# The experts' gate, x times sigmoid of 1.702 x, as one activation in place of a sigmoid and a product

## The chip, the cores and the metric

The kernel runs on one core of a Trainium2 chip. A core has a matrix engine (TensorE, PE in the profile; its weight loads are PEld) and three engines for the rest: VectorE (DVE), ScalarE (ACT) and GpSimd (POOL). SyncE (SP) issues most of the transfers (DMA). Each engine works through its own list of instructions in order and waits on semaphores for the others. The metric is the device time of one execution in microseconds (us), the median of several runs.

## The reference, cut to what matters

One encoder layer: attention, then a mixture of experts. 1024 tokens of width 1024 go to 4 of 32 experts each; every expert has a gate half and an up half of 1024 columns and a product back down. The part that the change touches is one line:

```python
def expert_block(args):
    xb, e = args
    gu = xb @ w_gate_up[e] + b_gate_up[e]
    gate = jnp.minimum(gu[:, :D_FF], SWIGLU_LIMIT)
    up = jnp.clip(gu[:, D_FF:], -SWIGLU_LIMIT, SWIGLU_LIMIT)
    glu = gate * jax.nn.sigmoid(SWIGLU_ALPHA * gate)      # SWIGLU_ALPHA = 1.702
    return ((up + 1.0) * glu) @ w_down[e] + b_down[e]
```

## The kernel before

The program runs in stages: projections and attention (to about 500 us), output projection and routing (to about 700), the experts (about 620 to 2240), and a final normalisation. The experts' first visit begins while the last tiles are still routed.

**Visits.** The experts are ranked by how many tokens they got, and a plan (PLAN) holds a capacity for each rank. Each expert is visited once or more. A visit of several blocks of 128 tokens is of kind H (`accH`, `xH`, `hH`), one of a single block of kind L (`accL`, `xL`, `hL`). The two streams are merged beforehand into one sequence of steps (`merged`), by estimated costs of TensorE and bytes moved. A step is a quarter of a 512-column piece of an expert's weights: kind "g" for gate and up columns, "d" for the product down.

**Weights.** SyncE loads two steps' weights at a time (L1181 for gate and up, L1184 for down). Most visits compute in a split form: a weight is "cooked" (`cook`) into a high part by ScalarE (L1305) and a low part, weight minus high part, which VectorE (736 of 1024 elements per partition, 368 of 512 columns twice) and GpSimd (the other 288) compute together (L1307). TensorE then does three products: high by high, high by low, low by high (L1532 to L1534 for wide visits, L236 to L238 for blocks over 64 tokens). So L238 and L1534 are the ones that need L1307. Blocks of up to 64 tokens alone take the weights as they are (L1557). Ten buffers hold raw and cooked weights; a load waits until L1307 has read the buffer before it.

**Gates.** In wide visits `glu_w` works on one quarter (j) of the columns with tokens along the row: VectorE adds the bias and clips (L1425, or L1422 and L1423 where high and low product lie side by side), ScalarE takes the sigmoid (L1428), VectorE multiplies it by the clipped gate (L1429). For the up half VectorE clips and multiplies (L1434) and the result is split again for the product down. In other visits `glu` does the same by blocks of 512 columns: L1449 and L1451 add, L1456 clips, L1457 is the sigmoid, L1458 the product, L1461 and L1462 the up half. `leave` scales a block's output (L1484, L1486 to L1489) and GpSimd adds it to the tokens' rows in memory (L1490).

**Order.** The source order is the input of a scheduler which simulates the program and sets each engine's list by that; the changed kernel is scheduled anew. SyncE's order is fixed by hand.

**Ranking.** `rank` (L1188 on) counts, sorts and writes the experts' order to `ord_i` (L1210); SyncE reads it before it can load the next experts' lists and weights. It runs on VectorE between the first visit's gates.

**The end.** A loop over leftover blocks (L1640), whose count is computed on the chip, is empty in this execution. `finish` loads tile i (L1709), squares it and takes a root on ScalarE (L1712, L1713), scales on VectorE (L1714, L1715) and stores (L1716). ScalarE's functions come in tables; a table load stands in its list where the function of the next instruction is in another one.

Of the kernel before, what the change touches and what calls it, by code (L numbers as in the profile page):

```python
# [9 lines left out]
AF = mybir.ActivationFunctionType  # L10
ALU = mybir.AluOpType
# [13 lines left out]
ALPHA = 1.702  # L25
# [48 lines left out]
def span(v):  # L74

    return sum(b[1] for b in v[2]) if len(v[2]) > 1 else 0


def joined(v):

    return 0 < span(v) <= 208


def groups(v, nt):

    return (0,) if nt > 64 else (0, 64) if nt > 32 else (0, 32, 64, 96) if plain(v) else (0, 32)
# [140 lines left out]
class Kernel:  # L227
# [1019 lines left out]
    def experts(self):  # L1247
# [3 lines left out]
        V, A, P, T = nc.vector, nc.scalar, nc.gpsimd, nc.tensor  # L1251
# [122 lines left out]
        def parts(name, n):  # L1374

            st, r, blocks = vis[n]
            if st == "H":
                t = wp.tile([128, 2 * KD * WIDE], F32R, name=name + st)  # L1380
            else:
                t = lp.tile([128, 2048], F32R, name=name + st)
            sp = span(vis[n])
            out, at = [], 0
            if plain(vis[n]):
                nt = blocks[0][1]
                w = t.bitcast(F32)[:, 0:KD * nt].rearrange("p (k t) -> p k t", k=KD)
                return w, [(w, w, None)]
            if sp and name == "x":
                w = t[:, 0:2 * KD * sp].rearrange("p (u k t) -> p u k t", u=2, k=KD)  # L1390
                return w, [(None, w[:, 0, :, o - blocks[0][0]:o - blocks[0][0] + nt],
                            w[:, 1, :, o - blocks[0][0]:o - blocks[0][0] + nt]) for o, nt in blocks]
            full = sum(b[1] for b in blocks if b[1] > 64)
            w = t[:, 0:2 * KD * full].rearrange("p (u k t) -> p u k t", u=2, k=KD) if full else None
            for o, nt in blocks:
                if nt > 64:
                    out.append((None, w[:, 0, :, at:at + nt], w[:, 1, :, at:at + nt]))
                    at += nt
                else:
                    lo = groups(vis[n], nt)[1]  # L1400
                    q = t[:, 2 * KD * full:2 * KD * full + KD * (lo + nt)].rearrange("p (k t) -> p k t", k=KD)
                    if nt < lo:
                        P.memset(q[:, :, nt:lo].bitcast(F32), 0.0)
                    out.append((q, q[:, :, 0:nt], q[:, :, lo:lo + nt]))
            return w, out
# [7 lines left out]
        def glu_w(n, c, j, p):  # L1413

            sp = span(vis[n])
            kk = 4 * (c // 2) + j
            bc = biases[n][:, 8 * (c % 2) + kk:8 * (c % 2) + kk + 1]
            top = LIM + c % 2
            t = wp.tile([128, 512], F32, name="t", bufs=3)[:, :sp]
            if joined(vis[n]):  # L1420
                A.activation(t, p[:, sp:2 * sp], AF.Copy)
                V.scalar_tensor_tensor(t, p[:, :sp], bc, t, op0=ALU.add, op1=ALU.add)  # L1422
                V.tensor_scalar(t, t, top, None, op0=ALU.min)  # L1423
            else:
                V.tensor_scalar(t, p[:, :sp], bc, top, op0=ALU.add, op1=ALU.min)  # L1425
            if c % 2 == 0:
                a = gates[n, j] = wp.tile([128, WIDE], F32, name="ga", bufs=5)[:, :sp]
                A.activation(a, t, AF.Sigmoid, scale=ALPHA)  # L1428
                V.tensor_tensor(a, a, t, op=ALU.mult)  # L1429
                return  # L1430
            if kk == 0:
                hs[n] = parts("h", n)
            a = gates.pop((n, j))
            V.scalar_tensor_tensor(a, t, 1.0 - LIM, a, op0=ALU.max, op1=ALU.mult)  # L1434
            w, blocks = hs[n]
            full = w.shape[3]
            self.split(w[:, 0, kk, :full], w[:, 1, kk, :full], a[:, :full])
            if full < sp:
                _, hi, lo = blocks[-1]
                self.split(hi[:, kk, :], lo[:, kk, :], a[:, full:])  # L1440

        def glu(b, p, c):

            nt = b["nt"]
            t = wp.tile([128, 512], F32, name="t", bufs=3)[:nt]
            c0 = 1024 * (c % 2) + 512 * (c // 2)
            bv = biases[b["n"]][:, c0:c0 + 512]
            *more, o = groups(vis[b["n"]], nt)
            V.tensor_tensor(t, p[o:o + nt], bv[o:o + nt], op=ALU.add)  # L1449
            for o in more:  # L1450
                V.tensor_tensor(t, p[o:o + nt], t, op=ALU.add)  # L1451
            if c % 2 == 0:
                if len(late) == 2:
                    settle(*late[0][1:3])
                a = b["a"] = lp.tile([128, 512], F32, name="a", bufs=3)[:nt]
                V.tensor_scalar(t, t, LIM, None, op0=ALU.min)  # L1456
                A.activation(a, t, AF.Sigmoid, scale=ALPHA)  # L1457
                V.tensor_tensor(a, a, t, op=ALU.mult)  # L1458
                return
            a = b.pop("a")  # L1460
            V.tensor_scalar(t, t, LIM, -LIM, op0=ALU.min, op1=ALU.max)  # L1461
            V.scalar_tensor_tensor(a, t, 1.0, a, op0=ALU.add, op1=ALU.mult)  # L1462
            if c == 1:
                hs[b["n"]] = parts("h", b["n"])

            late.append((self.pe_time + 5.0, b, c // 2, a))

        def settle(b=None, f=-1):

            for x in list(late):  # L1470
                if x[0] <= self.pe_time or (x[1] is b and x[2] <= f):
                    late.remove(x)
                    turn(x[3], hs[x[1]["n"]][1][x[1]["j"]][1:], x[1]["nt"], 4 * x[2])
# [32 lines left out]
        def mm(m):  # L1506
# [12 lines left out]
            if kind == "g" and span(vis[n]):  # L1519
                sp = span(vis[n])  # L1520
                x = xs[n][0]
                if kh == 0:
                    accs[n] = [bank() for _ in range(4)]
                for j in range(4):
                    ws = slice(128 * j, 128 * j + 128)
                    p = accs[n][j]
                    for k in range(KP):
                        kk = KP * kh + k
                        if joined(vis[n]):
                            mm(p[:, :2 * sp], hi[:, k, ws], x[:, :, kk, :], start=kk == 0, stop=False)  # L1530
                        else:
                            mm(p[:, :sp], hi[:, k, ws], x[:, 0, kk, :], start=kk == 0, stop=False)  # L1532
                            mm(p[:, :sp], hi[:, k, ws], x[:, 1, kk, :], start=False, stop=False)  # L1533
                        mm(p[:, :sp], lo[:, k, ws], x[:, 0, kk, :], start=False, stop=kk == 7)  # L1534
                    if kh == NP - 1:
                        glu_w(n, c, j, p)
                self.pe_time += pe_cost(vis[n], "g")
                settle()
                return
# [202 lines left out]
```

## Time and profile before

| | |
|---|---|
| time, median of 3 runs | 2270.0 us (2266.41 to 2276.21) |
| the profiled execution's own time | 2269.73 us |
| its span, first to last instruction | 2268.0 us |
| TensorE busy | 2084.2 us, 92% of the span |
| VectorE busy | 1568.2 us, 69% |
| ScalarE busy | 949.6 us, 42% |
| GpSimd busy | 1111.3 us, 49% |
| DMA | 579.17 MB, mean 255 GB/s |

The 1.7 us between span and time lie around the program. Busy shares are means over stages with different limits, and TensorE's busy time includes some of the time in which its pipeline waits; so what a part of a stage is worth is read in that stage. A line of idle time names who ended it. All rows are of one execution.

### The profile page before, as it was taken

To read this page: it belongs to the slowest core of one execution; us is meant where nothing else is said; L and a number is where in the kernel's file an instruction comes from. 1 tells how busy PE (TensorE), PEld (TensorE's weight loads), DVE (VectorE), ACT (ScalarE), POOL (GpSimd) and SP (SyncE) were. 2 spreads that over 40 slices of the span, in tenths; PEclk is the share of its full clock that TensorE was granted. 3 is DMA by queue.
4 is the path that set the end of the run, shared out by engine and by line. 5 is a ranking of instruction groups with operands and counts; after the bars stand their busy time and mean duration, and the time that the engine had idled before them with its cause. 6 is when DMAs were issued, how large, how long until landed. Compare 5 with 4: busy or idle time off the path is not lost. (4 is left out here: it accounts for less than half of the span.)

```text
span 2268.0 us, 34804 instructions
## 1 busy us (share of the span) xinstructions
PE 2084.2 (92%) x12090; PEld 1533.8 (68%) x12090; DVE 1568.2 (69%) x2790; ACT 949.6 (42%) x1612; POOL 1111.3 (49%) x959
## 2 busy tenths in 40 slices
PE   6999999999787998888879999999999999999973
PEld 3987777777576876665546555566686777877772
DVE  3777646876585699787866454455686868878975
ACT  3543436764353456554643121222233434345543
POOL 2522123543555567778874334333536455555453
PEclk8999999999899999999989999999999999999987
DMA  9555577823556699898879998999898898898775
GB/s 320 157 166 149 163 217 198 159 78 124 152 164 191 233 298 307 278 293 256 299 225 368 371 320 292 344 347 329 263 347 265 309 315 307 304 313 298 257 251 188
DMA packets 325114, 579.17 MB, mean 255 GB/s; under 512 B 40009, under 2 KB 78089, under 8 KB 322577
## 3 DMA queue, kind: packets, MB, share of 16 engines
q1 hardware_dynamic: 301529, 524.22, 67.7%
q0 software_dynamic: 23408, 52.71, 11.2%
q8 instruction: 97, 1.59, 0.3%
q14 instruction: 80, 0.66, 0.1%
HBM read 518.23 MB, written 58.92 MB: 254 GB/s over the span
## 5 line engine op out<-in xcount | busy, mean ns | idle before, releaser
L1307 POOL TENSOR_TENSOR w<-w,w 128x288 fp32r<-128x288 f32 x456 | 599.9, 1366 | 547.7 <-ACT w L1305 523.6
L1305 ACT ACTIVATE w<-w 128x1024 fp32r<-128x1024 f32 x456 | 469.1, 1054 | 525.3 <-DMA w<-in_w_gate_up 123.8
L1307 DVE TENSOR_TENSOR w<-w,w 128x736 fp32r<-128x736 f32 x456 | 504.8, 1119 | 214.1 <-ACT w L1305 211.9
L1534 PE MATMUL accH<-xH,w 128*128 128x256 f32 (+9 forms) x1408 | 396.8, 294 | 5.1 <-POOL w L1307 4.1
L1532 PE MATMUL accH<-xH,w 128*128 128x256 f32 (+6 forms) x1024 | 320.6, 316 | 2.2 <-ACT xH L243 0.6
L1533 PE MATMUL accH<-xH,w 128*128 128x256 f32 (+6 forms) x1024 | 315.2, 309 | 0.3 <-DVE xH L244 0.3
L1534 PEld LDWEIGHTS accH<-xH,w 128*128 128x128 f32 x1408 | 267.0, 191 | 18.3 <-POOL w L1307 4.8
L1532 PEld LDWEIGHTS accH<-xH,w 128*128 128x128 f32 x1024 | 193.0, 189 | 50.5 <-issue 27.4
L1533 PEld LDWEIGHTS accH<-xH,w 128*128 128x128 f32 x1024 | 193.7, 189 | 5.1 <-DVE xH L244 0.7
L1557 PE MATMUL accL<-w,xL 128*32 128x512 f32 (+3 forms) x896 | 176.9, 599 | 1.2 <-issue 0.8
L236 PE MATMUL accH<-w,hH 128*128 128x512 f32 (+3 forms) x368 | 150.1, 410 | 5.1 <-ACT w L1305 5.1
L237 PE MATMUL accH<-w,hH 128*128 128x512 f32 (+3 forms) x368 | 146.8, 399 | 0.0
L238 PE MATMUL accH<-w,hH 128*128 128x512 f32 (+3 forms) x368 | 143.2, 401 | 1.0 <-POOL w L1307 1.0
L238 PE MATMUL accL<-w,xL 128*72 128x512 f32 (+4 forms) x256 | 106.5, 416 | 39.9 <-POOL w L1307 28.6
L1530 PE MATMUL accH<-xH,w 128*128 128x416 f32 (+2 forms) x384 | 110.6, 365 | 10.1 <-DVE t L1422 10.0
L1490 POOL DMA_INDIRECT d_y<-y,lsH x54 | 96.6, 1789 | 45.6 <-DVE y L1484 32.9
L236 PE MATMUL accL<-w,xL 128*72 128x512 f32 (+4 forms) x256 | 104.3, 407 | 2.2 <-ACT w L1305 1.1
L1449 DVE TENSOR_TENSOR t<-accL,biasL 32x512 f32<-32x512 f32 (+8 forms) x88 | 60.5, 688 | 64.2 <-PE accL L1557 45.4
L236 PEld LDWEIGHTS accH<-w,hH 128*128 128x128 f32 (+3 forms) x368 | 68.4, 186 | 52.4 <-issue 19.2
L237 PE MATMUL accL<-w,xL 128*72 128x512 f32 (+4 forms) x256 | 103.4, 404 | 0.0
L1557 PEld LDWEIGHTS accL<-w,xL 128*32 128x32 f32 (+3 forms) x896 | 39.5, 115 | 84.6 <-issue 79.0
L237 PE MATMUL pm<-whi,hl 128*128 128x256 f32 x320 | 92.5, 290 | 1.4 <-DVE hl L244 1.2
(362 smaller groups left out, 4422.7 us busy)
## 6 DMA issues: line engine op xcount, KB each, us to landing
w<-in_w_gate_up SPq DMA_DIRECT2D x264, 1024.0 KB
w<-in_w_down SPq DMA_DIRECT2D x132, 1024.0 KB
aw<-in_w_ada SPq DMA_DIRECT2D x64, 256.0 KB
wraw<-in_w_in SPq DMA_DIRECT2D x18, 512.0 KB
xt<-in_x SPq DMA_DIRECT2D x16, 512.0 KB
wa<-in_w_ada SPq DMA_DIRECT2D x8, 1024.0 KB
d_h<-zero SPq DMA_DIRECT2D x9, 512.0 KB
d_y<-zero SPq DMA_DIRECT2D x18, 256.0 KB
```

The source lines that it names most:

```text
L236: mm(ps, lh, rh, start=start, stop=False)
L237: mm(ps, ll, rh, start=False, stop=False)
L238: return mm(ps, lh, rl, start=False, stop=stop).ins
L1305: A.activation(hi, w, AF.Copy)
L1307: eng.tensor_tensor(lo[:, :, cs], w[:, :, cs], hi[:, :, cs].bitcast(F32), op=ALU.subtract)
L1449: V.tensor_tensor(t, p[o:o + nt], bv[o:o + nt], op=ALU.add)
L1490: s = P.indirect_dma_start(out=self.d_y[c], out_offset=bass.IndirectOffsetOnAxis(ap=b["ls"][:nt, 0:1], axis=0), in_=y, in_offset=None, com ...
L1530: mm(p[:, :2 * sp], hi[:, k, ws], x[:, :, kk, :], start=kk == 0, stop=False)
L1532: mm(p[:, :sp], hi[:, k, ws], x[:, 0, kk, :], start=kk == 0, stop=False)
L1533: mm(p[:, :sp], hi[:, k, ws], x[:, 1, kk, :], start=False, stop=False)
L1534: mm(p[:, :sp], lo[:, k, ws], x[:, 0, kk, :], start=False, stop=kk == 7)
L1557: mm(p[o:o + nt], w[:, kk, :], hi[:, k, :], start=kk < len(at), stop=kk >= 8 - len(at))
```

## The change

In `glu_w` and in `glu` the pair of a sigmoid with scale 1.702 on ScalarE and a product on VectorE becomes one activation that gives x times sigmoid of 1.702 x. It writes the same tile. The loop of leftover blocks keeps its sigmoid and product (L1682, L1683).

```diff
             if c % 2 == 0:
                 a = gates[n, j] = wp.tile([128, WIDE], F32, name="ga", bufs=5)[:, :sp]
-                A.activation(a, t, AF.Sigmoid, scale=ALPHA)
-                V.tensor_tensor(a, a, t, op=ALU.mult)
+                A.activation(a, t, AF.Gelu_apprx_sigmoid)
                 return
...
                 a = b["a"] = lp.tile([128, 512], F32, name="a", bufs=3)[:nt]
                 V.tensor_scalar(t, t, LIM, None, op0=ALU.min)
-                A.activation(a, t, AF.Sigmoid, scale=ALPHA)
-                V.tensor_tensor(a, a, t, op=ALU.mult)
+                A.activation(a, t, AF.Gelu_apprx_sigmoid)
                 return
```

Line numbers of the changed kernel are one less from L1430 on and two less from L1459 on. The scheduler's lists change with it: VectorE's list loses the 132 products and many of its rows trade places with neighbours, ScalarE's gains two table loads, SyncE's stays the same. Three places follow.

VectorE in the ranking (`rw`, `rcol` are its small tables; `gT` and `yi` belong to the routing of the last tile). Before:

```order
L1208 COPY rcol<-pr 32x1
L1429 TENSOR_TENSOR ga<-ga,t 128x256
L1202 SCALAR_TENSOR_TENSOR rw<-lead_oh,rw 32x32
L1203 TENSOR_SCALAR rcol<-ip,lead_e 32x1
L1429 TENSOR_TENSOR ga<-ga,t 128x256
L1204 SCALAR_TENSOR_TENSOR rcol<-rcol 32x1
L1205 TENSOR_SCALAR rw<-rw,rcol 32x32
L1206 TENSOR_REDUCE rcol<-rw 32x1
L1307 TENSOR_TENSOR w_7576<-w_7408,w_7576 128x2x368
L1207 TENSOR_SCALAR rw<-ie,rcol 32x32
L1111 TENSOR_TENSOR gT<-pr,gT 32x128
L1210 CAST ord_i<-pr 1x32
```

and after:

```order
L1202 SCALAR_TENSOR_TENSOR rw<-lead_oh,rw 32x32
L1203 TENSOR_SCALAR rcol<-ip,lead_e 32x1
L1204 SCALAR_TENSOR_TENSOR rcol<-rcol 32x1
L1205 TENSOR_SCALAR rw<-rw,rcol 32x32
L1206 TENSOR_REDUCE rcol<-rw 32x1
L1207 TENSOR_SCALAR rw<-ie,rcol 32x32
L1307 TENSOR_TENSOR w_7568<-w_7404,w_7568 128x2x368
L1111 TENSOR_TENSOR gT<-pr,gT 32x128
L1210 CAST ord_i<-pr 1x32
```

The products are gone from the ranking, and L1207, on which a product of TensorE and then `ord_i` rest, stands ahead of the subtraction L1307.

VectorE in the second wide visit (456 tokens) beside a block of 72 tokens, about 1119 us. Before:

```order
L1456 TENSOR_SCALAR t<-t 72x512
L1307 TENSOR_TENSOR w_10933<-w_10865,w_10933 128x2x368
L1307 TENSOR_TENSOR w_10981<-w_10865,w_10981 128x2x368
L1429 TENSOR_TENSOR ga<-ga,t 128x456 x2
L1458 TENSOR_TENSOR a<-a,t 72x512
L1425 TENSOR_SCALAR t<-accH,biasC 128x456
L1307 TENSOR_TENSOR w_10994<-w_10880,w_10994 128x2x368
L1425 TENSOR_SCALAR t<-accH,biasC 128x456
L1307 TENSOR_TENSOR w_11004<-w_10880,w_11004 128x2x368
```

and after:

```order
L1455 TENSOR_SCALAR t<-t 72x512
L1307 TENSOR_TENSOR w_10904<-w_10837,w_10904 128x2x368
L1307 TENSOR_TENSOR w_10948<-w_10837,w_10948 128x2x368
L1425 TENSOR_SCALAR t<-accH,biasC 128x456 x2
L1307 TENSOR_TENSOR w_10961<-w_10852,w_10961 128x2x368
L1307 TENSOR_TENSOR w_10971<-w_10852,w_10971 128x2x368
```

Three products are gone from between two pairs of subtractions, and the two clips L1425 stand together ahead of the second pair.

ScalarE at the start of the final normalisation. Before:

```order
L1640 UNCONDITIONAL_BRANCH
L1712 ACTIVATE yj,ssf<-yf 128x1024
L1713 ACT_TABLE_LOAD
L1713 ACTIVATE ssf<-ssf,eps 128x1
L1712 ACTIVATE yj,ssf<-yf 128x1024
```

and after:

```order
L1638 UNCONDITIONAL_BRANCH
L1710 ACT_TABLE_LOAD
L1710 ACTIVATE yj,ssf<-yf 128x1024
L1711 ACT_TABLE_LOAD
L1711 ACTIVATE ssf<-ssf,eps 128x1
L1710 ACTIVATE yj,ssf<-yf 128x1024
```

A second table load stands ahead of the first tile's square.

## Rows read from the trace of the kernel before

**Rows 1.** Stretches: us, busy us (instructions) by engine, PE clock, DMA share, GB/s.
```profile
620.00:850.00 230.00, 196.16 (x1171) 172.25 (x1172) 172.41 (x297) 108.36 (x150) 137.34 (x115) 0.94 0.71 221
850.00:1250.00 400.00, 349.63 (x1562) 237.89 (x1561) 307.69 (x362) 203.81 (x239) 291.09 (x207) 0.96 0.88 290
1250.00:2050.00 800.00, 795.57 (x4561) 538.83 (x4561) 519.18 (x817) 248.08 (x358) 351.81 (x271) 1.00 0.93 314
2050.00:2244.00 194.00, 167.35 (x1006) 131.10 (x1004) 148.41 (x276) 90.27 (x171) 109.22 (x87) 0.95 0.72 242
```

**Rows 2.** Lines, 850 to 1250: count, busy us, mean ns, idle before, by releaser.
```profile
L1307 POOL TENSOR_TENSOR w<-w,w 128x288 fp32r<-128x288 f32 x175 | 243.3, 1478 | 84.8 <-ACT w L1305 80.5 <-DVE hH L244 3.0 <-DVE a L1458 0.6
L1307 DVE TENSOR_TENSOR w<-w,w 128x736 fp32r<-128x736 f32 x175 | 194.7, 1133 | 50.7 <-ACT w L1305 49.8
L238 PE MATMUL accL<-w,xL 128*72 128x512 f32 (+3 forms) x196 | 82.3, 420 | 35.6 <-POOL w L1307 26.3 <-DVE w L1307 9.1
```

**Rows 3.** One source line, whole span: durations in ns, min/median/max.
```profile
L1307 POOL TENSOR_TENSOR w<-w,w x456: 788/1442/7083, 624.0 to 2222.2; 128x288 fp32r<-128x288 f32 x152
```

**Rows 4.** Lines, whole span: the gates' sigmoids and products.
```profile
L1429 DVE TENSOR_TENSOR ga<-ga,t 128x256 f32<-128x256 f32 (+9 forms) x88 | 45.7, 543 | 2.4 <-ACT ga L1428 1.7
L1458 DVE TENSOR_TENSOR a<-a,t 32x512 f32<-32x512 f32 (+8 forms) x44 | 38.6, 878 | 11.2 <-ACT a L1457 11.2
L1428 ACT ACTIVATE ga<-t 128x256 f32<-128x256 f32 (+9 forms) x88 | 35.8, 429 | 73.0 <-DVE t L1425 55.0 <-DVE t L1423 17.9
L1457 ACT ACTIVATE a<-t 32x512 f32<-32x512 f32 (+8 forms) x44 | 27.6, 628 | 109.3 <-DVE t L1456 109.1
```

**Rows 5.** Lines by shape: a square of 512 columns on ScalarE.
```profile
L1019 ACT ACTIVATE ya<-xt 128x512 f32<-128x512 f32 x16 | 10.1, 631 | 34.4 <-POOL xt L1018 23.4 <-DVE xt L1018 11.0
```

**Rows 6.** Stretches of L1429 alone: us, DVE busy us (count), PE clock, DMA.
```profile
620.00:850.00 230.00, 8.86 (x16) 0.94 0.71 221
850.00:1250.00 400.00, 3.66 (x4) 0.96 0.88 290
```

**Rows 7.** Stretches of L1458 alone, the same columns.
```profile
620.00:850.00 230.00, 2.65 (x3) 0.94 0.71 221
850.00:1250.00 400.00, 14.11 (x15) 0.96 0.88 290
```

**Rows 8.** Timeline at 1122, VectorE and TensorE: start, us, instruction, idle before.
```profile
1121.96 2.42 DVE L1429 TENSOR_TENSOR ga<-ga,t 128x456 f32<-128x456 f32 x2
1124.31 1.27 DVE L1458 TENSOR_TENSOR a<-a,t 72x512 f32<-72x512 f32 x1
...
1127.16 0.65 PE L238 MATMUL accL<-w,xL 128*72 128x512 f32 x1 [2.78 <-DVE w L1307]
```

**Rows 9.** Timeline at 1180, VectorE, GpSimd and TensorE.
```profile
1180.01 1.29 DVE L1458 TENSOR_TENSOR a<-a,t 72x512 f32<-72x512 f32 x1
...
1181.42 9.36 POOL L1307 TENSOR_TENSOR w<-w,w 128x288 fp32r<-128x288 f32 x4 [0.66 <-ACT w L1305]
...
1188.56 0.70 PE L238 MATMUL accL<-w,xL 128*72 128x512 f32 x1 [6.12 <-POOL w L1307]
```

**Rows 10.** Timeline of VectorE at 686, in the ranking.
```profile
686.45 0.40 DVE L1429 TENSOR_TENSOR ga<-ga,t 128x256 f32<-128x256 f32 x1
...
688.51 0.93 DVE L1307 TENSOR_TENSOR w<-w,w 128x736 fp32r<-128x736 f32 x1 [1.09 <-ACT w L1305]
...
690.61 0.18 DVE L1210 CAST ord_i<-pr 1x32 int32<-1x32 f32 x1 [0.18 <-PE pr L1209]
```

**Rows 11.** Timeline at 2246, ScalarE and SyncE's queue, in the final normalisation.
```profile
2246.57 1.06 ACT L1712 ACTIVATE yj<-yf 128x1024 f32<-128x1024 f32 x1 [12.44 <-DMA yf<-d_y]
...
2247.74 1.28 ACT L1713 ACT_TABLE_LOAD   x1
2249.03 0.29 ACT L1713 ACTIVATE ssf<-ssf,eps 128x1 f32<-128x1 f32 x1
...
2251.25 1.30 SPq L1709 DMA_DIRECT2D yf<-d_y  x2
```

## The prediction, made before the changed kernel was run

> **What bounds the kernel now.** I read the table of stretches first [rows 1]: for each stretch of the expert stage it gives the busy time of TensorE (PE), of its weight loads, of VectorE (DVE), ScalarE (ACT) and GpSimd (POOL), then TensorE's granted clock, the DMA share and GB/s. The reader should see two kinds of stretch. From 1250 to 2050 us TensorE is busy 795.6 of 800.0 us at full clock (1.00, the level of 2.4 GHz): nothing that VectorE gives up can shorten it by more than the 4.4 us that are left. In the other three TensorE is idle for 230.0 - 196.2 = 33.8, 400.0 - 349.6 = 50.4 and 194.0 - 167.4 = 26.6 us, at a mean clock of 0.94 to 0.96, so part of each runs at the lower of the two levels, 1.2 GHz. Only there can a gain be had.
>
> Next I asked who TensorE waits for in the largest of them, 850 to 1250 us [rows 2]. Its biggest wait stands before L238, the product with the low part of a cooked weight: 26.3 us ended by GpSimd's L1307 and 9.1 by VectorE's. A weight is "cooked" by ScalarE (high part, L1305), and then VectorE and GpSimd subtract 368 and 144 of its 512 columns (L1307). VectorE is busy 307.7 of these 400 us and GpSimd 291.1 [rows 1]: neither is full, but they work through a fixed order in bursts, and TensorE stands behind the end of a burst. So a VectorE instruction taken from a burst is worth its whole length if TensorE waits for that burst's end, and nothing if it doesn't.
>
> **What goes.** The change takes out 88 of L1429 and 44 of L1458 on VectorE [rows 4]: 45.7 + 38.6 = 84.3 us of VectorE's time. VectorE also stood idle 11.2 us before L1458, waiting for the sigmoid; that wait can only move to the gate's next reader, L1462, which comes after another product, so I take it as gone with the rows. By stretch [rows 6, 7]: 8.9 + 2.7 = 11.6 us from 620 to 850, 3.7 + 14.1 = 17.8 us from 850 to 1250; the other 54.9 us lie behind 1250.
>
> **What is added.** L1428 and L1457 stay where they were, 88 and 44 times, with another function. No row shows that function. Its nearest rows are the other ScalarE activations of the same size: the sigmoid's mean is 628 ns for 512 columns [rows 4], and a square of 512 columns from SBUF takes 631 [rows 5]. Two functions with nothing in common differ by 3 ns. If the new one differed by as much, 132 of them would cost 0.4 us or give that back; I take 0. The order shows two more table loads on ScalarE. One stands in the loop of L1640, which runs no turn here. The other stands in the final normalisation.
>
> **The final normalisation, +1.3 us.** Before, ScalarE squares the first tile at 2246.57 after 12.44 us idle, then loads a table for the square root at 2247.74, 1.28 us [rows 11]. Now a load also stands ahead of that square, and it holds one of the square's two waits on the tile's halves. SyncE's queue explains why this counts: the store of tile 0 stands ahead of the loads of tile 6 (2251.25), so what delays tile 0 delays tile 6, tile 7 and the end. If the load ran inside the 12.44 us it would cost 0; behind the tile's last byte, 1.28. As it waits for a half of the tile, I take 1.3 and keep 0 as the other end.
> The Trainium skill (ScalarE: Activation LUTs, "What ACT_TABLE_LOAD costs") adds a drain of about 1.38 us to each load, 2.66 in all; by that this term would be an estimated 2.7 and the forecast 2260.4. The trace disagrees: behind the load of 2247.74 to 2249.02 the next activation starts at 2249.03 [rows 11].
>
> **620 to 850, -3 us.** Here the ranking of the experts shares VectorE with the first gates. SyncE can't load weights of the next experts before ord_i, 690.61 us [rows 10]. Four L1429 of about 0.40 us stand on VectorE between the mask of the last tile (mk) and ord_i, one of them at 686.45: 1.6 us earlier if the chain follows. The order also moves L1207 ahead of the subtraction that stood before it at 688.51; but ord_i itself still stands behind it, so I add nothing. Of the other 11.6 - 1.6 = 10.0 us I take a seventh, 1.4, as most of it lies beside products that TensorE has anyway. Ends: 0 and 11.6.
>
> **850 to 1250, -9 us.** At 1121.96 two L1429 (2.42 us) and an L1458 (1.27) run without a gap, some 3.7 us, and behind them TensorE stands 2.78 us for an L1307, until 1127.16 [rows 8]. All of the 2.78 can go. At 1180.01 an L1458 of 1.29 us stands in a burst behind which TensorE waited 6.12 us for GpSimd [rows 9]; 1.29 can go. So at these two places 2.78 + 1.29 = 4.07 of 4.98 us removed pay. They are the best places; L1458 also runs where no wait of TensorE follows. I take half of 17.8, rounded to 9. Ends: 0 (VectorE only waits longer for ScalarE, as it does for 49.8 us here [rows 2]) and 17.8.
>
> **1250 to 2244, 0 us.** Up to 2050 TensorE covers it. After 2050 it is idle 26.6 us, but the rows taken out (9.0 us) don't stand in the bursts that end its longest waits, which are made of L1307 alone. Ends: 0 and -4.4 up to 2050, 0 and -9.0 after.
>
> **The sum.** Against the profiled execution's own time of 2269.73 us, which is within 0.3 of the median: 2269.73 - 3 - 9 - 0 + 1.3 = 2259.0. Moving only the two large terms (the first between -1 and -5, the second between -5 and -13) its own range is 2253 to 2265.
>
> **Rivals.** *Nothing comes of it.* VectorE's freed time becomes idle time before L1307, since ScalarE's high part or the weight's transfer ends last. For it: VectorE already waits 49.8 us for ScalarE in the stretch [rows 2]. Against it: 1121.96, where VectorE had no gap [rows 8]. Time: 2269.73 + 1.3 = 2271.0.
>
> *GpSimd is relieved as well.* GpSimd's L1307 takes 788 ns at best and 1442 at the median [rows 3], 1478 in the mean from 850 to 1250 [rows 2]; in the burst of [rows 9] four take 9.36 us while VectorE runs on. So it waits for VectorE inside its instructions, 175 x (1478 - 788) ns = 121 us in that stretch. The removed rows are 17.8 of the 194.7 + 17.8 us that VectorE spends there on L1307 and on them, 8.4%; 8.4% of 121 is 10.1 us, on the path where TensorE waits for GpSimd. Time: 2259.0 - 10.1 = 2248.9.
> The Trainium skill has the mechanism (SBUF — State Buffer, "SBUF: two separate sides"): VectorE instructions with two SBUF inputs, as L1429 and L1458 are, and GpSimd's instructions hold one port pair in turn, each for its whole length. By that rule all removed rows count; the trace agrees that GpSimd stretches when VectorE has no gap.
>
> *Slower: GpSimd is starved longer.* Without the gates VectorE's subtractions stand closer together, and a GpSimd subtraction may wait for more of them in a row, as at 1181.42. Place: 850 to 1250; price: 6.12 us of TensorE each time [rows 9]. It decides from two more such waits on, the gains being eaten as in the first rival: 2271.0 + 2 x 6.12 = 2283.2. Against it: the removed rows hold GpSimd up as much as what moves into their place.
>
> That the change doesn't do what it says would need a table load between gates and plain copies; the order has none there, so this gets no chance.
>
> **How the numbers follow.** Forecast 0.48, nothing 0.23, GpSimd relieved 0.21, starved 0.08. A measurement here tells 0.5% from no change, that is 11.35 us: faster below 2258.65, slower above 2281.35. The forecast sits at that edge, so I split it 0.22 faster and 0.26 same. Faster: 0.22 + 0.21 = 0.43; same: 0.26 + 0.23 = 0.49; slower: 0.08. The range reaches from 5 us under the second rival to 2 us over the first, 2244 to 2273; it leaves out the starved case and the part of the relieved one beyond it.
>
> **What would show it.** VectorE's busy time should fall by about 84 us and L1307 keep its count. TensorE's idle time from 850 to 1250 should fall from 50.4 to about 41; if it stays at 50, nothing came of it; if it falls to 31 and GpSimd's mean there drops from 1478 towards 1350, GpSimd was relieved; if it rises with that mean, it was starved. ord_i should come some 1.6 us earlier. The last stage should show two table loads and last 1.3 us longer. The forecast is wrong if the new function takes longer per tile than the sigmoid's 429 and 628 ns, or if the stretch from 1250 to 2050 changes its length.

## The result

The changed kernel takes 2249.5 us (median of 6 runs, 2245.88 to 2257.16) against 2271.2 us of the kernel before beside it (6 runs, 2266.41 to 2276.21): ratio 0.9907, 95% interval 0.9886 to 0.9928, so 21.6 us or 0.9% faster. The forecast of 2259.0 had half of that gain; its range holds the time. The profiled execution took 2252.3 us, its span 2250.2.

The same stretches as in [rows 1], now of the changed kernel (us, busy us and instructions of PE, PEld, DVE, ACT and POOL, granted clock, DMA share, GB/s):

```profile
620.00:850.00 230.00, 198.56 (x1180) 173.96 (x1181) 165.19 (x278) 112.81 (x158) 142.46 (x117) 0.93 0.73 226
850.00:1250.00 400.00, 361.53 (x1636) 247.87 (x1635) 301.45 (x346) 205.86 (x242) 288.42 (x209) 0.97 0.93 305
1250.00:2050.00 800.00, 795.99 (x4603) 544.80 (x4602) 486.79 (x765) 255.06 (x374) 365.40 (x278) 1.00 0.93 315
```

From 850 to 1250 TensorE is idle 400.0 - 361.5 = 38.5 us where it was idle 50.4. The groups that answer [rows 2] and [rows 4] (line, engine, tiles, count, busy us, mean ns, idle us before by releaser), first from 850 to 1250 and then over the whole span:

```profile
L1307 POOL TENSOR_TENSOR w<-w,w 128x288 fp32r<-128x288 f32 x176 | 240.1, 1450 | 84.4 <-ACT w L1305 68.7 <-DMA w<-in_w_gate_up 8.1 <-DVE w L1307 4.1
L1307 DVE TENSOR_TENSOR w<-w,w 128x736 fp32r<-128x736 f32 x176 | 204.7, 1186 | 53.1 <-ACT w L1305 52.3
L238 PE MATMUL accL<-w,xL 128*72 128x512 f32 (+3 forms) x196 | 80.9, 414 | 23.0 <-POOL w L1307 14.0 <-DVE w L1307 9.1
```

```profile
L1428 ACT ACTIVATE ga<-t 128x256 f32<-128x256 f32 (+9 forms) x88 | 35.4, 428 | 63.7 <-DVE t L1425 45.5 <-DVE t L1423 17.7 <-ACT ga L1428 0.3
L1456 ACT ACTIVATE a<-t 32x512 f32<-32x512 f32 (+8 forms) x44 | 27.7, 629 | 117.3 <-DVE t L1455 117.2
```

TensorE's wait before L238 fell from 35.6 to 23.0 us, and nearly all of that at waits that GpSimd ended (26.3 to 14.0). The new function costs what the sigmoid did: 428 and 629 ns in the mean against 429 and 628.

**Both traces by the same work.** Windows at fixed times compare different work once one kernel runs ahead. So I follow single matmuls: the n-th product of a block, or the n-th of a wide visit, is the same work in every trace. For each of the two kernels there are two traces: before and before_again, after and both_loops (this one has the changed kernel's lists up to the leftover loop; see the experiments).

| part, by the matmuls that stood at these times in the first trace | before, before_again | after, both_loops | difference of the means | forecast |
|---|---|---|---|---|
| start to 851 | 851.1, 851.7 | 851.5, 850.9 | -0.2 | -3 |
| 851 to 1221 | 370.2, 375.4 | 354.6, 347.2 | -21.9 | -9 |
| 1221 to 2050 | 828.8, 829.2 | 826.6, 824.9 | -3.3 | 0 |
| 2050 to the last matmul | 182.7, 182.3 | 180.8, 181.4 | -1.4 | 0 |
| last matmul to the end | 35.2, 34.8 | 36.6, 36.4 | +1.5 | +1.3 |

The sum, -25.3, is up to rounding the difference of the spans' means; the medians say -21.6. Two executions of one kernel can differ by 10 us and more (the 30 of the kernel before beside two_inputs took 2256.87 to 2287.76), so a single row is good to some us. Nearly all of the gain lies in the one stretch from 851 to 1221.

### The profile page after: what moved, and what is told of

It reads as the page before. It is cut to its first block, busy times and chain, and to the rows that moved or that the text cites. A ratio compares the mean times of both kernels' runs of the same rounds, so it can differ in the third digit from the quotient of the medians.

```text
span 2250.2 us, 34684 instructions
## 1 busy us (share of the span) xinstructions
PE 2079.8 (92%) x12090; PEld 1537.3 (68%) x12090; DVE 1505.3 (67%) x2658; ACT 948.6 (42%) x1613; POOL 1109.1 (49%) x959
## 3 DMA queue, kind: packets, MB, share of 16 engines
q0 software_dynamic: 23408, 52.71, 11.2%
## 4 chain that ended last, share of the span: by engine, by line
PE 52%; DMA 15%; DVE 12%; issue 8%; POOL 6%; ACT 2%; SPq 1%; POOLq 0%; DVEq 0%; ACTq 0%
PE accL L1555 9%; DMA w<-in_w_gate_up 7%; PE accH L1530 5%; PE accH L1532 5%; PE accH L1531 5%; DVE w L1307 4%; POOL w L1307 4%; DMA w<-in_w_down 3%; PE accH L236 2%; PE accH L238 2%; PE accH L237 2%; PE poB L908 2%; PE pm L237 2%; PE pm L236 2%; PE pm L238 2%
## 5 line engine op out<-in xcount | busy, mean ns | idle before, releaser
L1307 POOL TENSOR_TENSOR w<-w,w 128x288 fp32r<-128x288 f32 x456 | 593.0, 1357 | 524.5 <-ACT w L1305 486.9
L1307 DVE TENSOR_TENSOR w<-w,w 128x736 fp32r<-128x736 f32 x456 | 515.6, 1143 | 233.9 <-ACT w L1305 227.9
L238 PE MATMUL accH<-w,hH 128*128 128x512 f32 (+3 forms) x368 | 142.8, 400 | 3.7 <-POOL w L1307 3.7
L238 PE MATMUL accL<-w,xL 128*72 128x512 f32 (+4 forms) x256 | 105.1, 411 | 26.4 <-POOL w L1307 16.4
```

The source lines that it names most:

```text
L238: return mm(ps, lh, rl, start=False, stop=stop).ins
L1307: eng.tensor_tensor(lo[:, :, cs], w[:, :, cs], hi[:, :, cs].bitcast(F32), op=ALU.subtract)
```

## The experiments

Each kernel was compared with runs of the kernel before on the same chip; in brackets stands the 95% interval of the ratio. Each is scheduled anew, TensorE's list included, and this limits what follows (last part of this section).

### VectorE's time, its port to SBUF, or the wait for the sigmoid: two_inputs and one_input

```diff
                 A.activation(a, t, AF.Gelu_apprx_sigmoid)
+                junk = wp.tile([128, 512], F32, name="junk", bufs=1)
+                V.tensor_tensor(junk[:, :sp], t, t, op=ALU.mult)       # two_inputs
...
+                junk = wp.tile([128, 1], F32, name="junk", bufs=1)
+                V.tensor_reduce(junk, t, axis=AX.X, op=ALU.max)        # one_input
```

The blocks' gates (`glu`) have the same line with `[:nt]`.

> The changed kernel, and behind each of the 132 new activations VectorE multiplies the clipped gate by itself into a tile that nobody reads: the removed products' shape and two SBUF inputs are back, without their wait for ScalarE. By the theory that what counts is VectorE's time in the bursts: about the time of before, 2266 to 2271 us. By the theory that the shared way of VectorE and GpSimd to SBUF counts: the same, 2266 to 2271, with GpSimd's L1307 as slow as before (1478 ns in the mean from 850 to 1250). By the theory that the wait for the sigmoid was what cost: about the time of after, 2250 us.

> The same kernel as two_inputs with the same order on every engine, but VectorE's extra instruction is a maximum along the row of the clipped gate: as many columns, one SBUF input, one column out. If VectorE's time in the bursts counts: 2266 to 2271 us, as two_inputs. If the shared way counts: near after, 2250 to 2256 us, and GpSimd's L1307 shorter than in two_inputs. If the wait for the sigmoid counts: 2250 us.

Measured: two_inputs 2270.1 us, ratio 0.9993 [0.9972, 1.0013]; one_input 2271.5, 0.9987 [0.9969, 1.0005]. Both are back at the time of before. The added rows of VectorE, of two_inputs and of one_input:

```profile
L1430 DVE TENSOR_TENSOR junk<-t 128x256 f32<-128x256 f32 (+9 forms) x88 | 50.1, 569 | 0.9
L1460 DVE TENSOR_TENSOR junk<-t 32x512 f32<-32x512 f32 (+8 forms) x44 | 34.2, 778 | 0.8
```

```profile
L1430 DVE TENSOR_REDUCE junk<-t 128x1 f32<-128x256 f32 (+9 forms) x88 | 38.2, 434 | 0.9
L1460 DVE TENSOR_REDUCE junk<-t 32x1 f32<-32x512 f32 (+8 forms) x44 | 29.6, 674 | 0.8
```

Neither row waits for ScalarE (0.9 and 0.8 us idle before them), yet the gain is gone: the 11.2 us of waiting before L1458 [rows 4] were worth nothing that can be measured. The instruction with one input takes less time than the one with two (434 and 674 ns against 569 and 778; it also writes one column only), and GpSimd's L1307 is shorter beside it, 1469 ns in the mean against 1516 from 851 to 1221. The Trainium skill (SBUF — State Buffer, "SBUF: two separate sides") says that VectorE's instructions with two SBUF inputs and GpSimd's hold one port pair in turn; these rows agree. But the time doesn't follow: with the same order on every engine, both kernels take the same. So neither the wait nor what the products do to GpSimd is worth anything that can be measured; what is left is VectorE's time, itself or by way of the lists that the scheduler makes for it. Even the time doesn't count evenly: one_input has 16.5 us less of it (67.8 against 84.3) and isn't faster.

### Is it the time or the list: tiny_inputs and product_and_dummy

```diff
-                V.tensor_tensor(junk[:, :sp], t, t, op=ALU.mult)
+                V.tensor_tensor(junk[:, :8], t[:, :8], t[:, :8], op=ALU.mult)       # tiny_inputs
...
-                A.activation(a, t, AF.Gelu_apprx_sigmoid)
+                A.activation(a, t, AF.Sigmoid, scale=ALPHA)                          # product_and_dummy
+                V.tensor_tensor(a, a, t, op=ALU.mult)
                 V.tensor_tensor(junk[:, :sp], t, t, op=ALU.mult)
```

> The kernel of two_inputs, but VectorE's 132 extra multiplications work on 8 columns, so that some 84 us of its time shrink to an estimated 10 or less while the count of instructions and their places in VectorE's list stay much as in two_inputs. If VectorE's time in the bursts is what counts: 2249 to 2255 us, close to after. If it is the list itself (how many instructions stand there and in which order the scheduler puts the others): 2262 to 2271 us, close to before.

> Sigmoid and product as before, and behind each product VectorE multiplies the clipped gate by itself into a tile that nobody reads: some 84 us more than before on VectorE. If VectorE's time in the bursts counts evenly: 21 us more than before, 2290 us (2283 to 2297). If the gain of the change came from one long wait that happened to lie behind its rows: 2275 us or less.

Measured: tiny_inputs 2254.3 us, 0.9924 [0.9902, 0.9945]; product_and_dummy 2287.1 us, 1.0073 [1.0050, 1.0096]. With 132 rows still in VectorE's list, but short, three quarters of the gain are there; with 80 us more of these rows than before, 16.6 us are lost. My estimate of the short rows was too low:

```profile
L1430 DVE TENSOR_TENSOR junk<-t 128x8 f32<-128x8 f32 x88 | 28.2, 320 | 1.2
L1460 DVE TENSOR_TENSOR junk<-t 32x8 f32<-32x8 f32 (+8 forms) x44 | 11.6, 264 | 0.9
```

39.8 us are left of 84.3, where I had estimated 10. From 39.8 us (tiny_inputs) to 84.3 (before, two_inputs) an us of these rows costs some 0.4 us, from there to 164.4 (product_and_dummy) some 0.2; the first 39.8, from after to tiny_inputs, cost 4 to 5 us in all, which isn't clear of the noise. It isn't one mechanism on both sides of before: of product_and_dummy's trace the part from 851 to 1221, where the change gains, takes 375.0 us against 370.2 and 375.4 before, and most of the loss stands behind 2050 (195 us to the last matmul against 182.5).

And the pair settles less than its heading asks. It shows that the number of rows in VectorE's list isn't what costs. But the scheduler knows how long the rows take, and TensorE's list goes with that: from 1120 to 1221 tiny_inputs has the changed kernel's list (7 of 343 matmuls stand elsewhere), two_inputs and product_and_dummy nearly before's (15 and 21 of 343). Short rows and the new list come together here.

### Which gates, and where: wide_only, block_only, late_only

```diff
+                if n > 0 and sp not in (312, 456):        # late_only; in glu: if nt < 72
+                    A.activation(a, t, AF.Gelu_apprx_sigmoid)
+                else:
+                    A.activation(a, t, AF.Sigmoid, scale=ALPHA)
+                    V.tensor_tensor(a, a, t, op=ALU.mult)
```

wide_only has the new activation in `glu_w` alone, block_only in `glu` alone.

> Only the wide visits' gates (88 of the 132, 45.7 us of VectorE's time before) have the new activation; the blocks' gates keep sigmoid and product. By the forecast's way of counting, TensorE's waits behind bursts are worth what is taken from each burst: from 620 to 1250 this takes out 12.5 of 29.3 us, so 43% of the gain: about 2262 us of before's 2271. If the one long wait of 1188 us, with only block products near it, makes most of the gain: 2265 us or more.

> Only the blocks' gates (44 of 132, 38.6 us and 11.2 us of idle time before) have the new activation; the wide visits keep sigmoid and product. By the forecast's way of counting it takes out 16.8 of 29.3 us from 620 to 1250, 57% of the gain: about 2259 us. If the long wait of 1188 us makes most of the gain: 2255 us or less.

> The new activation only in the visits whose gates lie behind 1250 us of before (wide visits of 428 tokens and less, blocks of 56 and less, 100 of the 132 products); sigmoid and product in the others. The forecast gave nothing to these: 2271 us, plus 1.3 for the table load in the final normalisation. If what the trace of after shows behind 1250 (some 4 us fewer) is of the change: 2267 us.

Measured: wide_only 2260.6 us, 0.9952 [0.9926, 0.9978]; block_only 2263.5, 0.9969 [0.9952, 0.9987]; late_only 2268.8, 0.9992 [0.9968, 1.0015]. The first two are near 2262 and 2259, where counting by rows put them, but in the other order: the blocks' gates should have given more and gave less, though the intervals overlap. They carry a cost that I hadn't seen: where sigmoid and the new function alternate, ScalarE loads a table at each turn. Of wide_only:

```profile
L1428 ACT ACT_TABLE_LOAD x17 | 21.8, 1283 | 0.3
L1456 ACT ACT_TABLE_LOAD x15 | 19.2, 1283 | 0.3
```

Before there are 2 such loads. So the two parts, measured at some 11 and 8 us, may each be worth more without these loads, and their sum needn't be the whole. late_only changes 92 of the 132 gates (its expectation says 100, a miscount) and gains nothing that can be measured, as forecast. That leaves the gain to the other 40, which but for four stand ahead of 1250; no run changed these alone.

### GpSimd's place in it: on_gpsimd, split_384, split_400

```diff
                 A.activation(a, t, AF.Sigmoid, scale=ALPHA)
-                V.tensor_tensor(a, a, t, op=ALU.mult)
+                P.tensor_tensor(a, a, t, op=ALU.mult)                               # on_gpsimd
...
-            for eng, cs in ((V, slice(0, 368)), (P, slice(368, 512))):
+            for eng, cs in ((V, slice(0, 384)), (P, slice(384, 512))):              # split_384
```

> Sigmoid on ScalarE as before, the product on GpSimd in place of VectorE: VectorE loses the same 84 us as in the change, GpSimd gets them. If only VectorE's time counts: near after, 2250 to 2255 us. If GpSimd's time counts as much, since TensorE waits longer for its L1307 (26.3 us) than for VectorE's (9.1): no gain or a loss, 2271 to 2290 us.

> The changed kernel with L1307 cut at column 384 in place of 368: VectorE gets 32 of 1024 elements more in each of 456 subtractions (estimated 456 x 33 ns = 15 us more), GpSimd 32 fewer (estimated at 788 ns for 288 elements: 456 x 88 ns = 40 us less). If GpSimd's time counts, as on_gpsimd says (84 us there and 84 us less on VectorE made 16 us, so some 0.4 us for each us), and VectorE's 0.2 to 0.25: 2249 - 16 + 4 = 2237 us. If the freed time of GpSimd is only waited away, since it waits for VectorE inside its instructions: 2249 to 2255 us.

> The same with the cut at column 400: by the same sums VectorE 30 us more and GpSimd 80 us less: 2249 - 32 + 8 = 2225 us if both count as above; 2255 to 2260 us if only VectorE's counts.

Measured: on_gpsimd 2286.3 us, 1.0065 [1.0042, 1.0087]; split_384 2242.0, 0.9866 [0.9842, 0.9889]; split_400 2251.2, 0.9911 [0.9889, 0.9934]. In on_gpsimd VectorE has lost the same rows as in the changed kernel, and the kernel is slower than before; on GpSimd the products take 75.7 + 66.0 us (mean 909 and 1500 ns) in place of the 84 that I had put down:

```profile
L1429 POOL TENSOR_TENSOR ga<-ga,t 128x256 f32<-128x256 f32 (+9 forms) x88 | 75.7, 909 | 27.2 <-ACT ga L1428 27.0
L1458 POOL TENSOR_TENSOR a<-a,t 32x512 f32<-32x512 f32 (+8 forms) x44 | 66.0, 1500 | 83.8 <-ACT a L1457 81.0 <-DMA w<-in_w_down 2.7
```

They are a load on either of the two engines that TensorE waits for, and a larger one on GpSimd. Whether their time there costs or that GpSimd, in its order, stands 27.2 and 83.8 us before them, mostly for the sigmoid, isn't separated. From 851 to 1221 its trace takes 373.1 us, as much as before: the gain of the change is gone there. The loss beyond that stands ahead of 851 (858.0 us; ScalarE loads 19 tables up to there against 17 before, and so it does in product_and_dummy) and from 1221 to 2050 (836 us against 829).

Cutting L1307 at 384 comes out between the two expectations (2237 and 2249), cutting it at 400 too (2225, and 2255 to 2260). Neither estimate of the engines' times held: GpSimd's hardly shrank with its columns, and VectorE's L1307 took 505.9 and 504.7 us, less than the 515.6 of the changed kernel, where I had estimated 15 and 30 more. Of split_384:

```profile
L1307 POOL TENSOR_TENSOR w<-w,w 128x256 fp32r<-128x256 f32 x456 | 583.5, 1322 | 536.6 <-ACT w L1305 523.5 <-DMA w<-in_w_down 3.2 <-DVE hH L244 2.8
```

With 256 elements in place of 288 the 456 subtractions take 583.5 us; in the changed kernel they took 593.0. I had estimated 40 us less. The shortest of them takes 717 ns, so by an estimate some 600 of the mean 1322 ns are waiting inside the instruction. Why these two kernels aren't slower than the changed one, and split_384 if anything faster, isn't shown. split_384 has the lowest median of all; beside both_loops, which ran on the same chip (2245.4, 0.9895 [0.9864, 0.9925]), the intervals overlap, so that it beats the changed kernel is likely and not shown.

### Do the waits repeat, and what the table load costs: before_again and both_loops

```diff
                     sg = rp.tile([128, 256], F32, name="sg", bufs=2)
-                    A.activation(sg, g[:, 0:256], AF.Sigmoid, scale=ALPHA)
-                    V.tensor_tensor(sg, sg, g[:, 0:256], op=ALU.mult)
+                    A.activation(sg, g[:, 0:256], AF.Gelu_apprx_sigmoid)            # both_loops
```

> The kernel before once more, to see how far the places of TensorE's waits repeat. If the long waits of 1127 and 1188 us belong to the kernel: they stand there again, and the stretch from the matmul of 1120 to that of 1221 takes some 101 us, as in the first trace. If they fell there by chance: the stretch takes 91 to 95 us, as in the runs with VectorE's time restored, and others take longer.

> The changed kernel with the new activation in the loop of leftover blocks too, which runs no turn here: the lists of all engines up to that loop stay the same, and the extra table load ahead of the first tile's square is gone. If that load is on the path, as forecast: the time from the last matmul to the end is 1.3 us shorter than in after (36.6 us), 35.3, and the whole time 2248. If it is hidden: 36.6 and 2249.5. The rest of the trace is a second look at after: about 101 us in the first visit and about 88 us from the matmul of 1120 to that of 1221.

before_again is one execution, of 2275.2 us. The waits of [rows 8] and [rows 9] stand again in it, some 10 and 6 us later; the stretch from 1120 to 1221 takes 96.9 us, between the two expectations (100.9 in the first trace). Its timeline of TensorE (start, us, instruction, idle before):

```profile
1137.48 0.67 PE L238 MATMUL accL<-w,xL 128*72 128x512 f32 x1 [2.79 <-DVE w L1307]
```

```profile
1188.23 0.40 PE L236 MATMUL accL<-w,xL 128*72 128x512 f32 x1
1188.47 0.40 PE L237 MATMUL accL<-w,xL 128*72 128x512 f32 x1
1194.16 0.70 PE L238 MATMUL accL<-w,xL 128*72 128x512 f32 x1 [5.29 <-POOL w L1307]
1194.65 0.63 PE L236 MATMUL accL<-w,xL 128*72 128x512 f32 x1
1195.08 0.63 PE L237 MATMUL accL<-w,xL 128*72 128x512 f32 x1
```

The last rows show what else a long wait costs: ahead of it a matmul starts every 0.23 us and takes 0.40, behind it every 0.43 and 0.63, which is the lower of the clock's two levels (1.2 GHz in place of 2.4). But the longer wait isn't fixed even where TensorE's list is: late_only has before's list in this stretch, row for row, and waits only 0.93 us at that matmul.

In the final normalisation the extra load of after stands where it was forecast, behind the wait for the tile. ScalarE of after, then of both_loops:

```profile
2227.81 1.28 ACT L1710 ACT_TABLE_LOAD   x1 [12.19 <-DMA yf<-d_y]
2229.10 1.06 ACT L1710 ACTIVATE yj<-yf 128x1024 f32<-128x1024 f32 x1
```

```profile
2218.98 1.06 ACT L1709 ACTIVATE yj<-yf 128x1024 f32<-128x1024 f32 x1 [12.50 <-DMA yf<-d_y]
2219.95 0.19 ACT L1709 ACTIVATION_READ_ACCUMULATOR yj<-yf 128x1 f32 x1
2220.15 1.28 ACT L1710 ACT_TABLE_LOAD   x1
```

From the end of ScalarE's wait to the end of the program the eight traces with two loads take 21.6 to 22.8 us, 22.3 in the mean, and the six with one load 21.3 to 22.2, 21.6 in the mean. So the load costs some 0.7 us: the sixth tile's square starts 9.42 us behind that point in all eight, against 8.13 to 8.60, but the last two tiles wait for their own transfers, which gives half back. The difference from 36.6 to 36.4 us in the table above (35.3 was expected of both_loops) doesn't show it, because the transfers ahead of the first tile vary by more (13.5 to 15.4 us from the last matmul to it).

### What stays open

The scheduler moves TensorE's rows too. Compared one by one by line and tile, at least 95 of the 1413 matmuls from 851 to 1221 have to change their place to turn before's order into the changed kernel's, 63 in the 343 from 1120 to 1221 alone. At the wait of 1188 it has put wide products and the turns of the gates' result (L1366) between the same two matmuls. TensorE of after there:

```profile
1171.31 0.39 PE L237 MATMUL accL<-w,xL 128*72 128x512 f32 x1
1171.54 0.37 PE L1532 MATMUL accH<-xH,w 128*128 128x456 f32 x1
...
1173.62 0.41 PE L1366 MATMUL pt<-idt,a 72*128 72x72 f32 x4
1173.83 0.44 PE L238 MATMUL accL<-w,xL 128*72 128x512 f32 x1
```

From 1120 to 1221 TensorE's lists are of two kinds. Seven traces have the changed kernel's but for 0 to 13 matmuls, seven have before's but for 0 to 21:

| list from 1120 to 1221 | us for that stretch, one execution each |
|---|---|
| the changed kernel's | split_384 84.4, both_loops 86.3, after 87.0, split_400 87.0, tiny_inputs 89.1, wide_only 95.3, on_gpsimd 98.0 |
| before's | two_inputs 90.6, late_only 93.4, one_input 94.2, before_again 96.9, block_only 97.7, before 100.9, product_and_dummy 102.2 |

The list alone doesn't make the gain: on_gpsimd and wide_only, which keeps the blocks' products on VectorE, have it and take 98.0 and 95.3 us. Shorter rows alone don't seem to make it either. block_only comes nearest to that: it has before's list but for 42 of the 1413 matmuls, and from 851 to 1221 its removed products leave VectorE as little busy as in after (276.6 us against 277.3; 284.9 before). It takes 368.2 us there, against 370.2 and 375.4 before and 354.6 and 347.2 in the changed kernel. But it has four table loads more in that stretch, and its traced execution was 8 us slower than its median. So the gain looks like both together, rows that are gone and a TensorE list that uses it; how they share it wasn't measured. No kernel here has the new activation with before's lists on every engine.

## Why the prediction was right or wrong

**What bounds the kernel: right.** The stretch from 851 to 1221 carries the gain; up to 851 and in the final normalisation there is none, and behind 1221 some 5 us.

**850 to 1250, -9 us: right place, the mechanism right in part, the term too small.** Measured by the same work it is -21.9 us, more than the 17.8 us that I had as the upper end. That an us taken from a burst pays if TensorE waits for its end holds at single waits (below); as the whole account it fails, since block_only takes 14.1 of the 17.8 us out and gains some 5 us there (with the reservations above). Three things were missing: I took half of the 17.8 us, and the idle time alone fell by 14.2; I counted no clock; and I took TensorE's list as given. The window over the same 1415 or so matmuls, of before_again and of both_loops:

```profile
851.74:1227.15 375.41, 325.43 (x1415) 224.55 (x1413) 290.33 (x326) 194.98 (x228) 283.88 (x201) 0.94 0.86 278
```

```profile
850.93:1198.14 347.21, 313.64 (x1416) 218.71 (x1414) 276.13 (x309) 194.81 (x228) 275.84 (x201) 0.98 0.92 301
```

Over the two pairs of traces TensorE's idle time falls from 50.2 to 36.0 us, by 14.2, and its busy time for the same matmuls from 322.6 to 314.9, by 7.7: with fewer long waits less of the stretch runs at the lower level (clock 0.94 and 0.96 before, 0.96 and 0.98 now). Not all of the 7.7 us need be the clock's: product_and_dummy has a clock of 0.95 there and is busy 316.7 us. The upper end of that term was no bound: I took it that an us removed can pay at most one. At 1127 the removal paid as forecast: the wait of 2.78 us is 0.44 now, and the burst of [rows 8] is a subtraction and two clips. At 1188 I allowed 1.29 of 6.12 us, and all of it went, with TensorE's new order (above); the forecast read the lists of VectorE and ScalarE only.

```profile
1120.43 1.28 DVE L1425 TENSOR_SCALAR t<-accH,biasC 128x456 f32<-128x456 f32 x2
1121.63 2.94 DVE L1307 TENSOR_TENSOR w<-w,w 128x736 fp32r<-128x736 f32 x2
...
1123.28 0.42 PE L238 MATMUL accL<-w,xL 128*72 128x512 f32 x1 [0.44 <-DVE w L1307]
```

These are VectorE and TensorE of after, at the place of [rows 8].

**620 to 850, -3 us: wrong.** The matmul of 851 comes at the same time in all four traces, and `ord_i` at 694.2 and 694.5 us against 690.6 and 694.1 before [rows 10], not 1.6 earlier. I had taken VectorE's rows as what sets `ord_i`; the wait of the subtraction that still stands ahead of it does. Of after, VectorE and then ScalarE:

```profile
689.40 0.29 DVE L1207 TENSOR_SCALAR rw<-ie,rcol 32x32 f32<-32x32 f32 x1
692.93 0.93 DVE L1307 TENSOR_TENSOR w<-w,w 128x736 fp32r<-128x736 f32 x1 [3.23 <-ACT w L1305]
694.19 0.18 DVE L1210 CAST ord_i<-pr 1x32 int32<-1x32 f32 x1
```

```profile
691.83 1.06 ACT L1305 ACTIVATE w<-w 128x1024 fp32r<-128x1024 f32 x1 [3.06 <-DMA w<-in_w_down]
```

VectorE is ready for that subtraction at 689.7 us, waits 3.23 us for ScalarE's high part, and ScalarE for the weight's transfer; in both_loops VectorE is ready at 687.0 and waits 6.22 us. Before it waited 1.09 us there [rows 10]. What delays that transfer wasn't followed.

**1250 to 2244, 0 us: about right.** -3.3 and -1.4 us from 1221 on, inside the ends that I gave (-4.4 and -9.0). late_only, which changes only these gates, doesn't show a gain, so some of it may be chance.

**The final normalisation, +1.3 us: right place, half the size.** 0.7 us; the last tiles' transfers give the rest back. The load itself is followed at once by the activation (2227.81 + 1.28 to 2229.10), so the drain which the Trainium skill adds (ScalarE: Activation LUTs, "What ACT_TABLE_LOAD costs") doesn't show here either.

**What is added, 0 us: right.** 428 and 629 ns.

**The rivals.** "Nothing comes of it" and "GpSimd is starved longer" fall with the time. "GpSimd is relieved as well" gave 2248.9, which is nearly the time measured, but by chance and not by its way. The waits that GpSimd ended did fall most (above), but GpSimd's L1307 should have dropped from 1478 towards 1350 ns and went to 1450, and between two_inputs and one_input, where it is relieved by 47 ns (1516 to 1469), the time doesn't move. VectorE's busy time fell by 62.9 us (1568.2 to 1505.3) and not by 84: its own L1307 took 515.6 us in place of 504.8, and other rows changed by a few us each.

## What to carry to other kernels

Where an engine off the path works in bursts that TensorE waits behind, count what it is relieved of in those bursts, and take the row's length neither as the upper end nor as the likely gain: a wait that goes can also give back what the lower clock costs behind it. If a scheduler plans the kernel, read the bottleneck engine's new list first, not only the lists of the engines that the edit touches. To learn whether a removed instruction cost by its time, its port or its dependency, put back one that has only one of the three, and look whether the bottleneck engine's list stayed the same.

## What I had not expected of the hardware

An instruction of VectorE on 8 columns costs 320 ns in the mean in wide visits, where the product on 144 to 456 columns took 543 [rows 4], and 264 in the blocks, where that on 512 took 878; at the median it is 166 and 156 ns, the rest of the mean comes from a few that take up to 2.4 us (tiny_inputs). The sigmoid and its product form are in different tables: alternating them costs a load of 1283 ns at each change (32 in wide_only). And a table load can carry the wait of the instruction behind it: in after it stood 12.19 us idle for a tile and then delayed the tile's square by its whole 1.28 us, though it reads nothing of the tile; some 0.7 us of that reach the end.
